# Masked softmax after a matmul: mask load moved behind two loads and W, unit 1 transposed early, TensorE fed zeros in the gaps

## Chip, cores, metric

One Trainium2 chip, one core. The metric is device time in microseconds (us) of one execution; most executions of one kernel agree within 0.3%. The profiles are of single executions; their span (89.1 us for the kernel before) is some 1.8 us shorter than the device time of the same run.

## The reference

```python
# x: (16, 512, 512) float32, weight: (512, 512), scale = 0.125
# mask: (np.triu(np.ones((512, 512))) == 0), so 1 strictly below the diagonal
y = scale * np.matmul(x, weight)
y = np.where(mask == 1, y, -1e9)
y_exp = np.exp(y - np.max(y, axis=-1, keepdims=True))
return y_exp / np.sum(y_exp, axis=-1, keepdims=True)
```

## The kernel before

The work is cut into 16 units of two half batches: 128 partitions, four rows of 512 in each, so that loading or storing a unit is one 1 MB transfer with 8 KB in one piece per partition. A unit is loaded, cast to bf16 by VectorE, transposed by TensorE (16 transposes), evicted from PSUM by VectorE and ScalarE, multiplied with W (4 x 4 matmuls, plus one that adds a band of -512 where the mask is 0), exponentiated by ScalarE with the row sum, scaled by VectorE and stored. Even units use only 256 columns. Of the mask only the four diagonal 128x128 blocks are read, 256 KB in rows of 512 B. All loads and stores go through one queue.

```python
load(0)
seq(nc.sync.dma_start(diag_f32, diag_r))                      # mask, 512 rows of 512 B
seq(nc.sync.dma_start(w_f32, weight.rearrange("(p kt) n -> p kt n", kt=KT)))
for u in range(1, X_BUFS):                                    # X_BUFS = 8
    load(u)

nc.vector.memset(zeros, 0.0)
idle = psum_y.tile([P, N], FP32, name="py")
for _ in range(WARM):                                         # 12 matmuls on zeros
    seq(nc.tensor.matmul(idle, lhsT=zeros[:, :P], rhs=zeros, start=True, stop=True))
# ... identity, constant parts of band and outputs, spread (cut) ...
cast(0)
seq(nc.vector.tensor_scalar(out=diag_bf, in0=diag_f32, ...))  # arguments cut
transpose(0)
evict(0)
for t in range(T):
    # spread matmul of diag_bf into PSUM, then two copies into band (cut)
    ...
seq(nc.vector.tensor_copy(w_bf[:, 0:2], w_f32[:, 0:2]))
seq(nc.scalar.copy(w_bf[:, 2:4], w_f32[:, 2:4]))
cast(1)

for u in range(U + 1):                                        # U = 16
    if u + 1 < U: transpose(u + 1)
    if u + 2 < U: cast(u + 2)
    if u + 1 < U: evict(u + 1)
    if u < U: multiply(u)
    if u >= 1:
        normalise(u - 1)
        store(u - 1)
        if u - 1 + X_BUFS < U: load(u - 1 + X_BUFS)
```

`seq` keeps the program order on an engine: an instruction that waits holds back all that follow it there.

The softmax here doesn't subtract the row's maximum and nothing guards it: scores larger than these inputs give would overflow.

## Time and profile before

| | kernel before |
|---|---|
| time, median of 3 runs | 90.88 us (90.73 to 90.93) |
| span of the profile | 89.1 us |
| PE busy | 72.0 us, 81% |
| DMA traffic | 34.87 MB in one queue, 16 engines 93.9% busy |
| last VectorE scaling ends | 81.96 us |
| last store: issued, landed | 82.0, 88.08 us |

The lines themselves, and how they are read, are in the prediction. A transfer called 1 MB has 1024 KB; the totals and the GB/s of the profile count in millions of bytes. Landing times here and below are the times in the trace at which a transfer's completion was counted. A transfer counts once for each of 16 DMA engines; "landed" means the last of them, "mean landing" the average of the 16.

### The profile page before, as it was taken

The page shows a single profiled execution, that of the slowest core. Times are in us where ns is not written, and L with a number is a line of the kernel's source. Part 1 is how long each engine was busy: PE and PEld are TensorE (multiplying, and loading weights), DVE is VectorE, ACT ScalarE, POOL GpSimd, SP SyncE. Part 2 cuts the span into 40 slices and gives each one's busy share as a digit, 9 for nine tenths or more (in the row PEclk, how much of TensorE's full clock was granted, in tenths as well). Part 3 has the DMA queues.
Part 4 walks back from the last instruction along what each step waited for, and adds up shares of the span by engine and source line. Part 5 has one row for each costly group of instructions (what it writes and reads, how often), then busy time and mean ns, then how long its engine had stood idle before and what let it go on. Part 6 is the DMA issues. An engine that isn't in the chain of part 4 may idle for free.

```text
span 89.1 us, 1610 instructions
## 1 busy us (share of the span) xinstructions
PE 72.0 (81%) x584; PEld 49.4 (56%) x592; DVE 60.5 (68%) x123; ACT 55.3 (62%) x154; POOL 7.3 (8%) x20
## 2 busy tenths in 40 slices
PE   4996205999999999999999999999999999960000
PEld 1325005767489569758955975795598578520000
DVE  5885914756849959994996899599685948607000
ACT  5403830646779778687977877797687869660000
POOL 7620000000100200020020002001000100200000
PEclk9999995559999999999999999999999999998555
DMA  0859999999999999999999999999999999999970
GB/s 11 324 204 381 419 434 427 423 423 430 416 419 419 423 430 430 419 419 423 423 427 430 430 416 419 430 434 423 416 427 430 419 416 430 438 416 434 423 313 22
DMA packets 5287, 34.95 MB, mean 392 GB/s; under 512 B 545, under 2 KB 1057, under 8 KB 1057
## 3 DMA queue, kind: packets, MB, share of 16 engines
q1 hardware_dynamic: 5280, 34.87, 93.9%
q8 instruction: 4, 0.07, 0.3%
q14 instruction: 3, 0.02, 0.0%
HBM read 18.09 MB, written 16.78 MB: 391 GB/s over the span
## 4 chain that ended last, share of the span: by engine, by line
PE 73%; DMA 12%; DVE 3%; SPq 2%; issue 1%; ACT 1%; DVEq 0%; ACTq 0%
PE py L118 48%; PE pt L94 16%; DMA xf<-in_x_dram 12%; PE py L127 8%; DVE ot L154 1%; DVE xb L85 1%; SPq L80 1%; ACT ot L137 1%; SPq L164 1%; SPq L165 1%; DVEq L264 0%; DVE rinv L152 0%; ACTq L264 0%
## 5 line engine op out<-in xcount | busy, mean ns | idle before, releaser
L118 PE MATMUL py<-w_bf,xt 128*128 128x256 bf16 (+1 forms) x248 | 51.0, 333 | 0.4
L137 ACT ACTIVATE ot<-py 128x256 f32<-128x256 f32 (+1 forms) x64 | 31.2, 493 | 8.9 <-PE py L127 8.8
L118 PEld LDWEIGHTS <-xt 128*128 128x128 bf16 x256 | 25.2, 101 | 12.7
L105 ACT COPY xt<-pt 128x1024 bf16<-128x1024 bf16 x16 | 16.2, 1013 | 14.7 <-PE pt L94 10.1
L154 DVE TENSOR_SCALAR ot<-ot,rinv 128x256 f32<-128x256 f32 (+1 forms) x64 | 23.5, 431 | 0.8
L85 DVE CAST xb<-xf 128x2048 bf16<-128x2048 f32 x16 | 19.5, 1220 | 5.9 <-DMA xf<-in_x_dram 5.9
L94 PE MATMUL pt<-ident_bf,xb 128*128 128x128 bf16 x256 | 17.8, 225 | 5.3 <-DVE xb L85 5.3
L94 PEld LDWEIGHTS <-xb 128*128 128x128 bf16 x256 | 16.6, 115 | 7.7 <-DVE xb L85 6.7
L127 PE MATMUL py<-band,ident_bf 128*128 128x256 bf16 x64 | 18.0, 281 | 0.0
L104 DVE COPY xt<-pt 128x1024 bf16<-128x1024 bf16 x16 | 11.0, 688 | 8.9 <-PE pt L94 8.9
L137 ACT ACTIVATION_READ_ACCUMULATOR ot<-py 128x1 f32 x64 | 12.8, 200 | 0.0
L156 POOL MEMSET ot<- 2x256 f32 x8 | 3.6, 448 | 67.7 <-DVE ot L154 67.7
L127 PEld LDWEIGHTS <-ident_bf 128*128 128x128 bf16 x64 | 6.5, 101 | 4.4
L173 PE MATMUL py<-zeros 128*128 128x512 bf16 x12 | 5.3, 632 | 1.2 <-DVE zeros L170 1.2
L152 DVE RECIPROCAL rinv<-rsum 128x4 f32<-128x4 f32 x16 | 2.7, 169 | 3.2 <-ACT ot L137 3.2
L179 DVE MEMSET ot<- 128x1024 f32 x4 | 3.6, 912 | 0.6 <-issue 0.6
L173 PEld LDWEIGHTS <-zeros 128*128 128x128 bf16 x12 | 1.6, 144 | 3.9 <-issue 2.8
L186 ACT ACT_TABLE_LOAD x1 | 1.3, 1283 | 0.7 <-PEq L250 0.7
L215 ACT CAST band<-py 64x256 bf16<-64x256 f32 x4 | 1.4, 368 | 0.2 <-DVE band L215 0.2
L215 DVE CAST band<-py 64x256 bf16<-64x256 f32 x4 | 1.4, 406 | 0.0
L208 PE MATMUL py<-diag_bf,spread 128*128 128x512 bf16 x4 | 1.0, 377 | 0.4 <-DVE diag_bf L194 0.4
L180 POOL MEMSET ot<- 2x256 f32 x4 | 1.2, 302 | 1.5 <-DVE ot L179 1.4
(14 smaller groups left out, 6.6 us busy)
## 6 DMA issues: line engine op xcount, KB each, us to landing
xf<-in_x_dram SPq DMA_DIRECT2D x16, 1024.0 KB, 13.9
out_dram<-ot SPq DMA_DIRECT2D x16, 1024.0 KB, 10.6
w_f<-in_weight_dram SPq DMA_DIRECT2D x1, 1024.0 KB, 8.4
diag_f<-in_mask_dram SPq DMA_DIRECT2D x1, 256.0 KB, 6.5
```

The costliest lines, as they stand in the source:

```text
L85: seq(nc.vector.tensor_copy(xb, st_x.pop(u)))
L94: nc.tensor.transpose(st_pt[u][kt // 2][:, kt % 2, t], xb[:, t].rearrange("p (k kt) -> p kt k", kt=KT)[:, kt], ident_bf,)
L104: seq(nc.vector.tensor_copy(xt[:, 0:2], pt[0]))
L105: seq(nc.scalar.copy(xt[:, 2:4], pt[1]))
L118: nc.tensor.matmul(py[:, :NC], lhsT=xt[:, kt, t], rhs=w_bf[:, kt, :NC], start=(kt == 0), stop=(kt == KT - 1),)
L127: nc.tensor.matmul(py[:, h * HB : NC], lhsT=ident_bf, rhs=band[:, h, t], start=False, stop=True, skip_group_check=True,)
L137: nc.scalar.activation(out=ot[:, t, :NC], in_=py[:, :NC], func=AF.Exp, bias=0.0, scale=float(scale), accum_out=rsum[:, t : t + 1],)
L154: seq(nc.vector.tensor_scalar_mul(ot[:, t, :NC], ot[:, t, :NC], rinv[:, t : t + 1]))
L156: seq(nc.gpsimd.memset(ot[0:2, 0, :HB], 1.0 / N))
L173: seq(nc.tensor.matmul(idle, lhsT=zeros[:, :P], rhs=zeros, start=True, stop=True))
L179: nc.vector.memset(ots[i][:, :, HB:], 0.0)
L215: seq(copy(band[half, :, t, g * P : (g + 1) * P], src[half, :, g]))
```

## The change

The intent: TensorE stands idle from 9.54 to 14.30 us, waiting for unit 1, and its granted clock then falls to one half. The mask is not needed before the multiplication. So it goes behind x0, W and x1; unit 1 is transposed while it lands, and zero matmuls fill the gaps so that the clock stays up.

```diff
-WARM = 12
...
     load(0)
+    seq(nc.sync.dma_start(w_f32, weight.rearrange("(p kt) n -> p kt n", kt=KT)))
+    load(1)
     seq(nc.sync.dma_start(diag_f32, diag_r))
-    seq(nc.sync.dma_start(w_f32, weight.rearrange("(p kt) n -> p kt n", kt=KT)))
-    for u in range(1, X_BUFS):
+    for u in range(2, X_BUFS):
         load(u)
...
-    idle = psum_y.tile([P, N], FP32, name="py")
-    for _ in range(WARM):
-        seq(nc.tensor.matmul(idle, lhsT=zeros[:, :P], rhs=zeros, start=True, stop=True))
+    def spin(n):
+        idle = psum_y.tile([P, N], FP32, name="py")
+        for _ in range(n):
+            seq(nc.tensor.matmul(idle, lhsT=zeros[:, :P], rhs=zeros, start=True, stop=True))
+    spin(12)
...
     cast(0)
+    transpose(0)
+    spin(16)
+    evict(0)
+    seq(nc.vector.tensor_copy(w_bf[:, 0:2], w_f32[:, 0:2]))
+    seq(nc.scalar.copy(w_bf[:, 2:4], w_f32[:, 2:4]))
+    cast(1)
+    transpose(1)
+    spin(8)
+    evict(1)
     seq(nc.vector.tensor_scalar(out=diag_bf, ...))           # arguments cut
-    transpose(0)
-    evict(0)
     for t in range(T):
         ...
-    seq(nc.vector.tensor_copy(w_bf[:, 0:2], w_f32[:, 0:2]))
-    seq(nc.scalar.copy(w_bf[:, 2:4], w_f32[:, 2:4]))
-    cast(1)
     for u in range(U + 1):
-        if u + 1 < U:
+        if 2 <= u + 1 < U:
             transpose(u + 1)
         if u + 2 < U:
             cast(u + 2)
-        if u + 1 < U:
+        if 2 <= u + 1 < U:
             evict(u + 1)
```

## The prediction

> **What bounds the kernel now.** I read the 40-slice strips of the page first, then the chain of work that ended last, then DMA shares in windows of 1 us at both ends of the span, then what VectorE waits for late. Strips of the kernel before:
>
> ```profile
> PE   4996205999999999999999999999999999960000
> PEclk9999995559999999999999999999999999998555
> DMA  0859999999999999999999999999999999999970
> GB/s 11 324 204 381 419 434 427 423 423 430 416 419 419 423 430 430 419 419 423 423 427 430 430 416 419 430 434 423 416 427 430 419 416 430 438 416 434 423 313 22
> ```
>
> A slice is 2.23 us. The DMA row is full from the fourth slice to the last but two, at a flat 416 to 438 GB/s; the PE row has a hole in slices 5 to 7 and is empty in the last four. The clock strip falls to 5 in slices 7 to 9, so TensorE ran its first real work at half clock. The chain view nevertheless gives 73% to PE:
>
> ```profile
> 2.63 10.36 DMA xf<-in_x_dram
> ...
> 14.30 1.89 PE pt L94 x16
> 16.19 0.85 PE py L118 x4
> ...
> 20.41 0.89 PE pt L94 x16
> ```
>
> The columns are start, duration, what. It says that unit 1's load, then 16 transposes (1.89 us at the low clock, 0.89 us at the full one) led to all that follows. Taken alone it promises that whatever PE saves before 20.41 us comes off the end. But the chain stops at the last VectorE scaling at 81.96 us, and the span is 89.1 us. What happens after it is in the DMA windows (columns: window, length, busy time of PE, PEld, DVE, ACT, POOL, clock, DMA share, GB/s):
>
> ```profile
> 5.00:6.00 1.00, 1.00 (x4) 0.30 (x2) 0.64 (x2) 0.00 (x0) 0.30 (x1) 1.00 0.59 194
> 6.00:7.00 1.00, 0.50 (x2) 0.00 (x0) 1.00 (x1) 0.00 (x0) 0.00 (x0) 1.00 0.39 96
> 7.00:8.00 1.00, 0.93 (x16) 0.93 (x17) 0.02 (x1) 0.00 (x0) 0.00 (x0) 1.00 1.08 415
> 20.00:80.00 60.00, 58.89 (x519) 42.06 (x524) 46.14 (x101) 47.15 (x136) 3.59 (x8) 1.00 1.01 424
> 84.00:85.00 1.00, 0.00 (x0) 0.00 (x0) 0.00 (x0) 0.00 (x0) 0.00 (x0) 0.50 1.03 434
> 86.00:87.00 1.00, 0.00 (x0) 0.00 (x0) 0.00 (x0) 0.00 (x0) 0.00 (x0) 0.50 0.41 172
> ```
>
> The queue still moves 434 GB/s two us after the last computation. Totals agree: 34.87 MB on the queue at 424 GB/s are 82.2 us; the first packet starts at 2.2 us; the dip at 5 to 7.5 us and the slow first packets cost about 1.7 us; the last packet ends at 87.7 us because some engines finish 1.5 to 2 us behind the average; the span ends 1.4 us later. 2.2 + 82.2 + 1.7 + about 1.6 + 1.4 = 89.1. The trace's completions of successive 1 MB transfers also stand 2.45 us apart right to the end (83.21, 85.63, 88.08 us). Last, VectorE in 60 to 82 us:
>
> ```profile
> 63.55 1.23 DVE L85 CAST xb<-xf 128x2048 bf16<-128x2048 f32 x1 [0.78 <-DMA xf<-in_x_dram]
> 68.42 1.23 DVE L85 CAST xb<-xf 128x2048 bf16<-128x2048 f32 x1 [0.96 <-DMA xf<-in_x_dram]
> ```
>
> The casts of units 14 and 15 already wait for their loads (landing at 63.53 and 68.40 us). So compute has caught up with the transfers by then. My reading: **the one DMA stream is the bound**, and PE is nearly co-critical but not the end.
>
> **What the Trainium skill says.** "Perfetto Trace Analysis", What "DMA-bound" means, puts such a kernel on specific DMA engines or on the issuing sequencer. The trace shows the first: share 1.01 at 424 GB/s, while the issuing instructions take only about 0.6 us each. "DMA: Bandwidth & Descriptors", Specifications, gives a fabric ceiling of 435 GB/s; the windows touch 434, so there is nothing to win in the steady state. Its section Why small descriptors are slow charges a fixed cost to each descriptor; here the mask is 512 rows of 512 B and moves at 96 GB/s in the 6 to 7 us window, which agrees. "TensorE: Matmul & The Clock Gate", Part 1, says that PE falls to half clock after an idle window of about 3.4 us; PE was idle 9.54 to 14.30 us and the granted clock is 0.5 from 13.4 to 20.2 us, which agrees.
>
> **The change part by part.** It removes no work and adds 24 zero matmuls; bytes and number of transfers are the same.
>
> Transfers. Old order: x0, mask, W, x1, x2; completions 5.77, 8.01, 10.51, 12.99, 15.48 us. New order: x0, W, x1, mask, x2. With 2.48 us a MB and the mask's own 2.24 us (8.01 - 5.77): W 8.25, x1 10.7, mask 13.0, x2 15.5. After the mask the stream stands where it stood. Its 2.24 us are not all needed: of each engine's 32 small packets most took 27 ns, 32 x 27 = 0.86 us, yet an engine spent 1.7 to 2.1 us on them, with pauses of about 0.4 us after the first two and again in the middle. If those pauses came from descriptors not yet ready early in the run, three MB ahead would hide them, worth up to 1.0 to 1.3 us. If they belong to short packets as such, nothing is won. I give the first a third: mean 0.4 us.
>
> PE and VectorE at the start. Spin 12 ends near 6.5 us as before; transposes of unit 0 from 7.1 to 8.1 us; 16 zero matmuls x 0.216 us (512 columns at the full clock, twice the 256-column pace of the L118 matmuls) = 3.5 us, to 11.6; cast(1) 10.7 to 12.0 us (1.23 us); transposes of unit 1 to 13.1 us (16 in 1.06 us); 8 zeros x 0.216 = 1.7 us, to 14.9. VectorE evicts unit 1 (0.69) to 14.0, then makes diag_bf (0.43) to 14.5. So the four spread matmuls wait for the 8 zeros, not for the mask, run to about 16.0 us, and the band casts (4 x 0.35 us) end near 16.9. multiply(0) starts at about 16.0 (before: 16.0, after its L94 group), at full clock, and takes about 2.2 instead of 4.2 us, ending near 18.5; the first later transpose comes at 18.5 instead of 20.4. **PE gains about 1.9 us**; the last multiply would end at 77.4 instead of 79.3 us. The last two loads still land at about 63.5 and 68.4 us, so the gain thins there to 1 to 1.9 us.
>
> What it buys at the end. The last store is issued at 80 to 81 instead of 82.0 us, behind a queue that is already full; the store took 6.1 us from issue to landing, against 2.45 for its own megabyte. It will wait longer, and land where the stream's length puts it: 88.08 minus the 0.4 us. Sum: 90.88 - 0.4 = **90.5 us**.
>
> **The rivals.** (a) PE is the bound, as the 73% say, and its 1.9 us come off: 89.0 us. For it: the chain, and the last store's issue following the last scaling. Against it: the full DMA row and 82.2 us of transfers. I hold it unlikely. (b) The mask gets cheap behind the megabytes and the stream shortens by 1.0 to 1.3 us: 89.6 to 89.9. For it: the pauses inside the mask packets; against: they look like the price of short rows. (c) The new prologue runs late (16 + 8 zeros stand in program order before needed work): if multiply(0) ended 2 us later than before, the first store would issue at 25 us instead of 23.05, with loads queued to about 29 us: the stream would not run dry, so 90.9. Only some 6 us of delay would show. (d) The laggard DMA engine. The end is the slowest of 16 engines; completion of x6 came 3.86 us after that of x5 around an instruction fetch of 1.10 us at 23.9 us. 48 more PE instructions move these fetches in time; that can win or lose 0.5 to 1.4 us by where they fall.
>
> **Range and chances.** The centre is 90.5. Down, (b) and a luckier (d) reach 89.4; up, an unluckier (d) 91.1. Faster by over 2% means below 89.06 us: it needs (a), or (b) and (d) together; 5%. Slower by over 2% (above 92.7) would need the stream to run dry or two bad fetches on one engine; 2%.
>
> **What would show it right or wrong.** Right: the clock strip has no 5s before the end; PE's last matmul ends 1 to 2 us sooner; yet the DMA row is as full, the last store takes 7 to 8 us to land, and the last landing is within 1 us of 88.08. The low-share dip moves from 5 to 7.5 us to about 10.5 to 13 us; its depth decides (b). The casts of units 14 and 15 wait for DMA longer than 0.78 and 0.96 us. Wrong: the last store landing earlier by as much as PE does means (a); a DMA share well under 1 between 15 and 80 us means a dry stream.

## The result and the profile after

The changed kernel takes **90.97 us** (median of 4 runs, 90.79 to 91.10) against 90.91 us (90.73 to 91.02) for the kernel before on the same chip. The ratio is 1.0008 with a 95% interval of 0.9984 to 1.0032: the same. A ratio here is the mean time of one kernel's fast runs over that of the other's fast runs of the same rounds, so it is not quite the ratio of the medians. Executions over 1.5% slower than the fastest of the same kernel are left out of the means.

The strips of the changed kernel, to be laid beside those in the prediction (a slice is again 2.23 us):

```profile
PE   4967979899999999999999999999999999700000
PEclk9999999999999999999999999999999999995555
DMA  1899779999999999999999999999999999999970
GB/s 22 313 408 431 293 289 438 419 431 419 427 419 431 419 431 419 416 419 431 423 427 412 434 427 423 423 431 423 419 416 445 416 427 419 434 419 427 434 316 33
```

All that the change intended is there. The hole in the PE row is gone, the clock strip has no 5 until PE has finished, and the PE row ends a slice earlier. The DMA row is as full as before. Its dip has only moved, from the third slice to the fifth and sixth (293 and 289 GB/s), where the mask now stands. The first digits of PEclk are not to be trusted: up to about 5 us the zero matmuls follow each other at 0.43 us, in both kernels, and the later ones of the changed kernel at about 0.22 us.

The chain of waits of the changed kernel (start, duration, what):

```profile
2.07 8.88 DMA xf<-in_x_dram
10.97 1.24 DVE xb L84
12.26 1.08 PE pt L93 x16
13.34 1.73 PE py L175 x8
18.53 0.89 PE pt L93 x16
```

The transposes of unit 1 take 1.08 instead of 1.89 us and start 2.0 us earlier; the first transposes of the main loop start at 18.53 instead of 20.41 us. Those 1.9 us are there again at the end of the computation, as the last eight stores show in the queue's own timeline, first before, then after (start of the first, time to the end of the last issue):

```profile
54.98 27.55 SPq L160 DMA_DIRECT2D out_dram<-ot  x8
```

```profile
53.11 27.55 SPq L159 DMA_DIRECT2D out_dram<-ot  x8
```

The first and the last of these issues come 1.87 us earlier, the last one at 80.12 us. Between them the gain goes and comes back: the fourth store is issued 0.2 us earlier and the fifth 0.1 us later than before, behind the casts that wait for the last two loads. But the last store **landed at 88.05 us, against 88.08** before. It took 7.9 us from issue to landing instead of 6.1. VectorE shows the stream as the pace setter once more, in the casts of the last two units:

```profile
63.62 1.23 DVE L84 CAST xb<-xf 128x2048 bf16<-128x2048 f32 x1 [1.75 <-DMA xf<-in_x_dram]
68.51 1.23 DVE L84 CAST xb<-xf 128x2048 bf16<-128x2048 f32 x1 [1.27 <-DMA xf<-in_x_dram]
```

They start 0.1 us later than before, after waits of 1.75 and 1.27 us where it was 0.78 and 0.96.

### The profile page after: what moved, and what is told of

Its sections match the earlier page's. It is cut to its first block, busy times and chain, and to the rows that moved or that the text cites. A ratio compares the mean times of both kernels' runs of the same rounds, so it can differ in the third digit from the quotient of the medians.

```text
span 89.1 us, 1666 instructions
## 1 busy us (share of the span) xinstructions
PE 74.3 (83%) x616; PEld 50.0 (56%) x616; DVE 60.3 (68%) x123; ACT 55.0 (62%) x154; POOL 7.3 (8%) x20
## 4 chain that ended last, share of the span: by engine, by line
PE 72%; DMA 10%; DVE 4%; SPq 1%; ACT 1%; DVEq 0%; issue 0%; ACTq 0%
PE py L117 47%; PE pt L93 15%; DMA xf<-in_x_dram 10%; PE py L126 8%; PE py L175 2%; DVE ot L153 1%; DVE xb L84 1%; SPq L79 1%; ACT ot L136 1%; SPq L163 1%; DVE band L226 0%; DVEq L272 0%; ACT band L226 0%; PE py L219 0%; DVE rinv L151 0%
## 5 line engine op out<-in xcount | busy, mean ns | idle before, releaser
L117 PE MATMUL py<-w_bf,xt 128*128 128x256 bf16 (+1 forms) x256 | 49.4, 326 | 0.3 <-ACT band L226 0.3
L117 PEld LDWEIGHTS <-xt 128*128 128x128 bf16 x256 | 24.4, 98 | 12.6 <-issue 0.5
L153 DVE TENSOR_SCALAR ot<-ot,rinv 128x256 f32<-128x256 f32 (+1 forms) x64 | 23.5, 431 | 0.8
L93 PE MATMUL pt<-ident_bf,xb 128*128 128x128 bf16 x256 | 17.0, 219 | 1.7 <-DVE xb L84 1.7
L93 PEld LDWEIGHTS <-xb 128*128 128x128 bf16 x256 | 15.9, 114 | 3.6 <-DVE xb L84 2.7
L126 PE MATMUL py<-band,ident_bf 128*128 128x256 bf16 x64 | 17.4, 273 | 0.0
L175 PE MATMUL py<-zeros 128*128 128x512 bf16 x36 | 10.3, 447 | 1.2 <-DVE zeros L170 1.2
L175 PEld LDWEIGHTS <-zeros 128*128 128x128 bf16 x36 | 3.9, 112 | 6.3 <-issue 2.7
L190 ACT COPY spread<-ident_bf 128x128 bf16<-128x128 bf16 x4 | 1.0, 330 | 0.2 <-POOL ident_bf masks.py:199 0.2
```

What stands on the lines that cost most here:

```text
L93: nc.tensor.transpose(st_pt[u][kt // 2][:, kt % 2, t], xb[:, t].rearrange("p (k kt) -> p kt k", kt=KT)[:, kt], ident_bf,)
L117: nc.tensor.matmul(py[:, :NC], lhsT=xt[:, kt, t], rhs=w_bf[:, kt, :NC], start=(kt == 0), stop=(kt == KT - 1),)
L126: nc.tensor.matmul(py[:, h * HB : NC], lhsT=ident_bf, rhs=band[:, h, t], start=False, stop=True, skip_group_check=True,)
L153: seq(nc.vector.tensor_scalar_mul(ot[:, t, :NC], ot[:, t, :NC], rinv[:, t : t + 1]))
```

## The experiments

Theory: the stream of transfers sets the end, so time follows what is done to the stream, and a faster prologue on PE only gives slack. Rivals: PE sets the end, and something ate its gain; or the mask's place in the queue matters. Twelve kernels ran, in three calls of four, each beside the kernel before on the same chip (medians of that: 90.98, 90.85 and 90.86 us).

The runs at a glance, without the two that store less. "Mean landing of x3" says how long the first part of the stream was (5.25 MB in most runs); the kernel before has 17.62 us, the changed kernel 17.61 us. In e4 and e5 the queue ran dry later on; the medians of e6 and e12 include two slow runs each, their ratios do not.

| run | mean landing of x3 | last store landed | time, median | ratio to before |
|---|---|---|---|---|
| changed kernel | 17.61 | 88.05 | 90.97 | 1.0008 |
| e1_one_block | 15.98 | 87.66 | 90.14 | 0.9895 |
| e2_two_masks | 18.72 | 89.32 | 92.12 | 1.0123 |
| e3_no_late_spin | 17.69 | 88.35 | 91.04 | 1.0003 |
| e4_long_spin | 17.53 | 91.00 | 93.78 | 1.0315 |
| e5_act_queue | 17.32 | 91.75 | 93.59 | 1.0318 |
| e6_act_queue_old | 17.35 | 87.71 | 91.59 | 1.0015 |
| e10_blocks_spread | 17.42 | 87.97 | 90.63 | 0.9977 |
| e11_blocks_in_row | 17.52 | 88.05 | 90.92 | 1.0007 |
| e12_spread_no_spin | 17.33 | 88.36 | 91.59 | 1.0044 |
| e13_old_order_blocks | 17.57 | 88.09 | 90.90 | 1.0000 |

### e1_one_block: a shorter stream

```diff
-    seq(nc.sync.dma_start(diag_f32, diag_r))
+    seq(nc.sync.dma_start(diag_f32[:, 0], mask[0:P, 0:P]))
```

and diag_bf is made from block 0 four times (the blocks are equal for this input, so the result is right).

> The changed kernel, but only the first 128x128 block of the mask is loaded (64 KB, 128 rows of 512 B) and used for all four blocks, which are equal for this input, so the result stays right. Theory (the one DMA stream sets the end, and short rows cost what they cost wherever they stand): the mask's 2.19 us in the stream shrink to some 0.5 us, so the last landing moves from 88.05 to about 86.4 us and the time from 90.97 to about 89.3 us, with PE's last matmul unchanged at about 77.4 us. Rival (PE or the chain of waits sets the end): time unchanged at 90.9, as PE waits for the 8 zero matmuls, not for the mask.

Measured: ratio 0.9895 (0.9862 to 0.9929), median 90.14 us. Faster by 1%, clear of the noise, as the theory says, but by half of what was expected. The four runs fall into two groups, 89.83 and 89.86, 90.41 and 90.44 us; the profile is of the slowest. In it the stream is 1.63 us ahead up to x6 (mean landing 23.52 against 25.15 us) and only 0.96 us ahead at x7 (26.67 against 27.63): between 23.5 and 25.5 us many packets of x6 and x7 took 0.5 to 1.5 us instead of 0.31. One straggling engine then ended 1.55 us behind the mean, in the changed kernel 1.09. Why these packets were slow is not settled; presumably the faster pair of runs had no such stretch, but there is no trace of those. PE's end was as in the changed kernel, so the rival that PE sets the end is out: less data in the stream alone brought the time down.

### e2_two_masks: a longer stream

```diff
     seq(nc.sync.dma_start(diag_f32, diag_r))
+    seq(nc.sync.dma_start(diag_2, diag_r))
```

> The changed kernel with the same mask load done a second time into a tile that nobody reads, right behind the first. Theory (stream): another 2.2 us of short rows in the stream, last landing near 90.25 us, time about 93.1 us, all the rest as in the changed kernel. Rival (PE sets the end): the second load holds back no PE work before unit 2, time 91.0 or a little more.

Measured: ratio 1.0123 (1.0104 to 1.0142), 92.12 us, that is +1.15 us over the changed kernel. The second mask, which nobody reads, lengthened the stream by 1.11 us (mean landing of x3 18.72 against 17.61 us), and the mean landing of the last store moved by the same 1.09 us, from 86.96 to 88.05. The last VectorE scaling began only 0.5 us later (78.94 us). **In this run the time follows the stream one to one**; in e1 the mean landing of the last store moved by 0.85 us and the median by 0.83. What I had wrong is the price of the second mask: 1.1 us, not 2.2. Short rows do not cost a fixed amount each: the two masks together took 2.9 us, of which the first had landed 0.8 us after x1 and the second 2.1 us after the first.

### e3_no_late_spin: the new order alone

```diff
-    spin(16)
...
-    spin(8)
```

> The changed kernel with the 16 and the 8 zero matmuls left out: the new order alone. Theory: TensorE's clock falls to half in one of its windows again, multiply(0) and the transposes of unit 2 come 1.5 to 2.5 us later than in the changed kernel (at 20 to 21 instead of 18.4 us), the last store is issued near 82 instead of 80 us, and the last landing stays at 88.0 to 88.1: time 90.9 within 0.3. Rival (PE sets the end): time up by the same 1.5 to 2.5 us.

Measured: ratio 1.0003 (0.9987 to 1.0019), 91.04 us. The time is as expected, but PE lost nothing, against what I wrote. Clock strip and last scaling of this run:

```profile
PEclk9999655899999999999999999999999999996555
```

```profile
78.44 1.67 DVE L153 TENSOR_SCALAR ot<-ot,rinv 128x512 f32<-128x512 f32 x4
```

The low clock fell into slices 5 to 8, from about 9.6 to 16.4 us, where little more than 16 transposes and 4 spread matmuls runs (1.90 and 1.86 us instead of 1.08 and 1.03). multiply(0) started at 16.02 us (16.19 us with the zeros); its first four matmuls took 0.79 instead of 0.60 us, all later ones ran at the full clock, and the last scaling began at 78.44 us, as in the changed kernel (78.41). In this run the gain of 1.9 us was the order's alone. The low clock simply lay earlier. For a run where it falls later, see e12.

### e4_long_spin: how much slack there is

```diff
-    spin(16)
+    spin(44)
```

> The changed kernel with 44 instead of 16 zero matmuls, which delays multiply(0) and all PE work after it by about 28 x 0.216 - 0.5 = 5.5 us. Theory: the stream keeps the end as long as the last store is issued early enough to land in its turn. It would be issued at about 80.1 + 5.5 = 85.6 us, and a lone 1 MB store needs some 4.5 us to land, so the last landing comes near 90.1: time about 93.0, that is +2.0 and not +5.5; the stream itself hardly runs dry. This measures the slack that the change added to and that my prediction put at some 6 us: if it is 6 us, the time stays at 91.0. Rival (PE sets the end): +5.5, 96.5 us.

Measured: ratio 1.0315 (1.0291 to 1.034), 93.78 us, +2.8 us for a delay of PE of 5.3 us (last scaling begins at 83.68 instead of 78.41 us). So neither +5.5 (PE) nor 0 (my 6 us of slack). The DMA windows show where the stream gave way (window, length, busy PE, PEld, DVE, ACT, POOL, clock, DMA share, GB/s):

```profile
26.00:27.00 1.00, 1.00 (x7) 0.52 (x6) 1.00 (x3) 0.72 (x3) 0.00 (x0) 1.00 0.83 344
27.00:28.00 1.00, 1.00 (x7) 0.49 (x6) 0.49 (x1) 0.72 (x3) 0.00 (x0) 1.00 0.38 156
28.00:29.00 1.00, 1.00 (x15) 0.79 (x13) 0.00 (x0) 0.71 (x3) 0.00 (x0) 1.00 1.09 451
29.00:30.00 1.00, 1.00 (x16) 0.93 (x14) 0.90 (x3) 0.73 (x3) 0.00 (x0) 1.00 1.26 344
30.00:31.00 1.00, 1.00 (x12) 0.90 (x10) 1.00 (x3) 1.00 (x4) 0.00 (x0) 1.00 0.71 180
```

The first store was issued at 26.44 us (21.50 in the changed kernel) and the eight first loads were used up at about 26.5 us: the queue stood nearly dry for about 1.3 us. Two stretches of slow packets followed (344 and 180 GB/s at 29 to 31 us, 229 to 303 at 36 to 39). By its end the stream was 2.9 us behind (mean landing of the last store 89.87 against 86.96 us). Counted against 424 GB/s, an estimate, the thin windows at 26 to 28 us lost 0.8 us and the two slow stretches 1.9 us. So the dry queue itself explains less than a third of the delay. The slow stretches came after it here and at the same times in e5, whose queue also ran dry; that the one brings the other is not shown. What is shown: the cost arises in the middle of the stream. I had expected it at the other end, from the last store.

### e5_act_queue and e6_act_queue_old: the mask from ScalarE's queue

```diff
-    seq(nc.sync.dma_start(diag_f32, diag_r))
+    seq(nc.scalar.dma_start(diag_f32, diag_r))
```

once in the changed kernel (e5), once in the kernel before (e6). Both then have the same stream of transfers.

> The changed kernel with the mask issued from ScalarE's queue at the start, so that its short rows run beside the megabytes instead of holding a place in the one stream. Theory (stream sets the end; in the trace of the changed kernel each engine spent 1.9 us on 32 rows of 27 ns, so more than half of that is pause which other packets could fill): the stream gets 0.9 to 1.1 us shorter, time near 90.0 us; x0 lands up to 0.9 us later and PE's end stays within 1 us of 77.4 us. Rival (the pauses are time in which an engine can do nothing else): time 90.9 as now. Rival (PE sets the end): 90.9 or later by the delay of x0.

> The kernel before, with only the mask moved to ScalarE's queue; old order of work, no late zero matmuls. The stream is then the same as in the other run with the mask on ScalarE's queue. Theory (stream sets the end): the same time as that run within 0.3 us, near 90.0, though PE's end may be 1 to 2 us later. Rival (the order of work on PE matters for the end): slower than that run by the 1.9 us that PE differs.

Measured: e5 ratio 1.0318 (1.0284 to 1.0352), 93.59 us; e6 ratio 1.0015 (0.9968 to 1.0063), median 91.59 us over all six runs, of which four count as fast (90.45, 90.49, 91.51, 91.67) and two as slow. All expectations but the rival on delay failed. The mask's packets did not share an engine's time with x0's: they ran from 1.85 us on, and x0's first packet came at 3.69 us in e5 and 3.86 us in e6, instead of 2.17 and 2.19 us. From then on about as many 8 KB packets were under way as engines had finished their part of the mask (8 at 4.5 us, 13 at 5.25 us in e5), so it looks as if each engine moved all its mask rows first. x0 landed at 8.90 us, 3.0 us later than with the mask behind it. The stream's mean landing of x1 was 12.35 and 12.38 us, against 12.65 us for x1 before and 12.61 us for the mask after (the same bytes each time): 0.25 us gained, not 1.0.

The two differ by 3% though their streams are the same up to then. Here is PE in e5:

```profile
10.21 1.90 PE L93 MATMUL pt<-ident_bf,xb 128*128 128x128 bf16 x16 [4.17 <-DVE xb L84]
11.90 5.49 PE L175 MATMUL py<-zeros 128*128 128x512 bf16 x16
...
21.12 0.60 PE L117 MATMUL py<-w_bf,xt 128*128 128x256 bf16 x4 [0.26 <-ACT band L226]
```

PE waited 4.2 us for x0 and lost its clock; the 16 zero matmuls, which were to keep it, ran mostly at half clock (5.49 us instead of 3.62) and stood in program order before the transposes of unit 1. multiply(0) started at 21.1 us, the first store was issued at 26.1 us, and the stream stood dry as in e4, with slow stretches after it at the same times (229 and 303 GB/s at 29 to 31 us, 246 to 311 at 36 to 39; the mean landing step from x7 to the first store is 3.9 us, where 2.5 is the rule). In e6, without those zeros, multiply(0) started at 16.7 us. So the zeros, harmless in the changed kernel, are a risk when the loads are late. The four fast runs of e6 fall into two pairs 1.1 us apart; the profile is of the faster pair, and the difference is not explained.

### e8 and e9: with the stream out of the way

Each even unit stores only half of its rows, 4.2 MB less in the stream. Their outputs are wrong, which doesn't matter for the times.

```diff
-        seq(nc.sync.dma_start(out_r[u // 2, u % 2], ot.rearrange("p t n -> p (t n)")))
+        if u % 2 == 0:
+            seq(nc.sync.dma_start(out_r[u // 2, 0, :, :, : 2 * N], ot[:, :2].rearrange("p t n -> p (t n)")))
+        else:
+            seq(nc.sync.dma_start(out_r[u // 2, u % 2], ot.rearrange("p t n -> p (t n)")))
```

> The kernel before, but of every even unit only the first half of the rows of a partition is stored (512 KB instead of 1 MB; result wrong on purpose). It takes 8 x 0.52 MB = 4.2 MB or 9.9 us out of the stream, so that compute must become the bound. Theory: the last store is issued at about 82 us as before and lands some 4.5 us later; time about 89.3 us, to be compared with the next run.

> The changed kernel with the same halved stores (wrong on purpose). Theory: with the stream out of the way PE's earlier end shows at last: 1.7 to 2.0 us less than the kernel before with halved stores, about 87.4 us. Rival (the change never gave PE anything that counts, or something else than the stream eats it): the two kernels with halved stores take the same time within 0.4 us.

Measured: the kernel before with halved stores 87.86 us (ratio 0.9692, 0.9651 to 0.9732), the changed kernel with halved stores 87.19 us (0.9587, 0.9572 to 0.9602). The intervals don't touch: **with the stream out of the way** (98 GB/s at 78 to 80 us in e9) **the change is faster**, by 0.7 us in the medians and by 1.0 us in the ratios (0.0105 of 90.85). That is half or less of the 1.7 to 2.0 us expected, and more than the rival's 0.4. The queue's timeline has the last store of each, e8 first:

```profile
80.89 0.54 SPq L163 DMA_DIRECT2D out_dram<-ot  x1
```

```profile
80.10 0.54 SPq L162 DMA_DIRECT2D out_dram<-ot  x1
```

They landed at 85.10 and 84.30 us: 4.2 us after their issue in both, so here the 0.8 us between the issues are the 0.8 us between the ends. That it is 0.8 and not 1.9 us is, in this pair of profiles, the clock's doing: in e8's the low clock hardly touches the first multiplications, and the last scaling begins at 79.19 us instead of 80.29 us in the kernel before. Where the low clock fell in the other runs of e8 no trace shows. The gain of the change on PE is thus not a constant; it depends on where the low clock falls.

### e10 to e13: the shape of the mask's load

Four loads of one 128x128 block each instead of one load of all. e10 puts them between the big loads, e11 in a row in the changed kernel's place, e13 in a row in the old kernel; e12 is e10 without the late zeros. The core of e10 (block c is `mask[c * P : (c + 1) * P, c * P : (c + 1) * P]`):

```diff
     load(0)
+    <block 0>
     seq(nc.sync.dma_start(w_f32, ...))
+    <block 1>
     load(1)
-    seq(nc.sync.dma_start(diag_f32, diag_r))
-    for u in range(2, X_BUFS):
+    <block 2>
+    load(2)
+    <block 3>
+    for u in range(3, X_BUFS):
         load(u)
```

> The changed kernel with the mask's four 128x128 blocks as four loads of 64 KB (8 rows of 512 B for each engine) that stand between the big loads: x0, block 0, W, block 1, x1, block 2, x2, block 3, x3. Right for any mask that the kernel before is right for. A single block took 0.22 us of the stream in the one-block run, four in one load 1.91 us. Theory A (an engine pauses when many short rows follow each other): four times 0.22 is 0.9 us, the stream ends 1.0 us earlier, time near 89.9. Theory B (the cost goes with the number of rows): the same 1.9 us in all, time 90.9.

> The changed kernel with the mask as the same four 64 KB loads, one behind the other in the old place of the mask. If what costs is many short rows in succession, it takes 1.9 us as before and the time stays at 90.9; if what costs is one load with many rows, it takes 0.9 us and the time is near 89.9, as with the blocks spread out.

> The blocks spread out, and the 16 and 8 zero matmuls left out: the candidate for a better kernel. As the zero matmuls bought nothing when taken out alone (91.04 against 90.97 us), I expect the time of the blocks spread out within 0.3 us, near 89.9 if theory A of that run holds, PE's end within 1 us of 77.4 us.

> The kernel before with only the mask's load cut into the same four 64 KB loads, in a row in its old place. Separates the shape of the load from the order of the work: the stream theory expects the same gain (or none) against the kernel before as the blocks in a row show against the changed kernel, within 0.4 us, although PE works in the old order and its end is up to 1.9 us later.

Measured: e10 90.63 us, ratio 0.9977 (0.9965 to 0.9989); e11 90.92 us, 1.0007 (0.9994 to 1.002); e13 90.90 us, 1.0000 (0.9988 to 1.0012). So theory B comes closer: these 512 rows cost nearly the same in one load, in four in a row, or spread out, in the old place or the new one. A fixed price for each row it is not (e2). In e10 the time from x0's to x3's mean landing is 11.79 us; four megabytes at 2.485 us are 9.94, so the blocks took 1.85 us. My 0.22 us for a block was read too narrowly: it is the step to the block's own landing, and part of its cost shows in the next load's. e10 is the fastest right version for a general mask, by 0.2%.

e12 is the surprise: 91.59 us over six runs, of which two, 92.35 and 93.35 us, count as slow (ratio of the four fast ones 1.0044, 1.001 to 1.0079; that of e10, with the zeros, ends at 0.9989). The fastest run, 90.76 us, has the highest mean granted clock, 0.934; the other fast ones, 91.16 to 91.89 us, have 0.917 to 0.920. Clock strip and end of its profiled run (91.16 us):

```profile
PEclk9999755559999999999999999999999999999955
```

```profile
82.00:84.00 2.00, 0.00 (x0) 0.00 (x0) 0.75 (x2) 0.00 (x0) 0.00 (x0) 1.00 0.77 324
```

The last block arrives 2 us later than the mask did, the low clock now falls on multiply(0) (three of its four groups of matmuls take 1.02 to 1.06 instead of 0.60 us), and the last scaling begins at 81.08 us. The last store is issued at about 82.8 us, and just before its data come the stream has a hole of a quarter (324 GB/s in 82 to 84 us, 426 in the changed kernel). So here the zeros do have a use: they keep the slack when the low clock falls badly.

## Why the prediction was right

The measured 90.97 us lies in the range, near its upper end of 91.1; the centre was 0.5 us too low.

- **What bounds the kernel**: right. Adding to the stream and taking from it moved the time (e2, e1); earlier PE work left it alone (the change, e3, e13); with the stream shortened by 4.2 MB, PE's earlier end showed (e8, e9). PE work that comes much later does count, once the queue runs dry (e4, e5).
- **The stream's landings**: W, x1, mask, x2 were given as 8.25, 10.7, 13.0 and 15.5 us and came at 8.45, 10.95, 13.14 and 15.62. That the mask might become cheap behind three megabytes, my third of a chance and the 0.4 us in the sum, failed: its step in the stream was 2.19 us instead of 2.24, and the last landing moved by 0.03 us. This is the term that made 90.5 of what was 90.97. The prediction also called the mask's 96 GB/s an agreement with a fixed cost for each descriptor. It agrees in direction only: a row took 27 ns, 32 of them 0.86 us of the 1.9 us, and the rest is pauses; and in e2 the second mask cost 1.1 us, not 1.9. Why an engine pauses stays open.
- **PE at the start**: right to 0.2 us or so (multiply(0) at 16.19 us for 16.0, the next transposes at 18.53 us for 18.5, 1.9 us gained). The zeros took 3.62 and 1.89 us for 3.5 and 1.7. What I credited to the warm clock was in e3's run the order's work.
- **What it buys at the end**: right; 7.9 us from issue to landing, where 7 to 8 were named. The gain did not thin to 1 to 1.9 us, though: it was all but gone at the fourth and fifth of the last eight stores and whole again, 1.87 us, at the last.
- **Rival (c), the slack**: the step "loads queued to about 29 us ... only some 6 us of delay would show" failed. The queue was used up at 26.5 us in e4, not at 29 (29.1 is when the last of 16 engines had counted x7), and a delay of 5.3 us against the changed kernel, 3.4 us against the kernel before by the first store's issue (26.44 to 23.05), cost 2.8 us, under a third of it in the dry queue itself. At the end of the stream the slack is smaller still: in e12 an issue at 82.8 us, 0.8 us later than in the kernel before, left a hole.
- **Rival (d), the laggard engine**: the jump that stood between x5 and x6 (3.86 us, instruction fetch at 23.9 us) stood between x4 and x5 in the changed kernel (20.59 to 24.29 us, fetch at 20.8 us). The sum was the same. The first fetch came between 20.6 and 25.7 us in the 14 traces, and in each of them it is a load under way at that time that needed 2.57 to 2.59 us in mean landing instead of 2.48: the jump moves with the fetch. No run takes the fetch away, so that the fetch causes the jump is argued, not shown.
- **Small misreadings**, without effect on the sum: the fourth slice moved 381 GB/s, not 416 to 438; unit 0's transposes (1.09 us) ran at the full clock, so the low clock hit unit 1's and multiply(0), not all the first real work; the 0.89 us of 16 later transposes is the chain's share of 1.06 us, so 1.89 against 1.06 is the clock's effect.

## What to carry to other kernels

Read what happens after the chain's last piece of compute: when a full queue outlives it, an engine's share of the chain is no promise, and less in the queue shortens the kernel: here 192 KB less gave 0.8 us (e1), the same bytes in another shape at most 0.2 us (e10). Time saved on an engine behind such a queue becomes slack, which may still be worth having where the time depends on something that varies from run to run, here the clock. In e4 the slack ran out where the queue first got empty; that is to be read from when the queue's packets end, not from when the last engine of a transfer reports.

## What the Trainium skill lacked or had wrong

- "DMA: Bandwidth & Descriptors", Specifications, gives 512 B as the size from which a transfer runs at line rate. Here 512 rows of 512 B moved at 96 GB/s in the 6 to 7 us window, in a queue that does 424, and took 1.7 to 2.2 us for 256 KB in every place and shape tried, two such loads back to back 2.9 us. A row alone took 27 ns, which is 19 GB/s for an engine (an estimate) where 8 KB in 0.31 us are 26; the rest is pauses between rows.
- "TensorE: Matmul & The Clock Gate", Part 4, says that the full clock does not engage for transposes. 16 transposes took 1.90 us at half clock (e3) and 1.06 to 1.09 us at the full one, so they do run at it where it is granted. Whether transposes alone would bring it up no run shows.
- No page gives what the fetch of instructions does to a full queue: 16 KB pieces of 0.9 to 1.1 us, four or five per execution, the first of them beside a load that takes 2.57 to 2.59 us in mean landing instead of 2.48.
- None says how a stretch of slow packets arises in a stream of 8 KB pieces (0.5 to 1.5 us instead of 0.31 in e1, 180 GB/s in e4, and at the same times in e5); the runs leave it open.
